# The norm factors of three stages: a transposing DMA of 16-bit halves in place of two TensorE transposes each

## The chip, the cores and the metric

The kernel runs on one core of a Trainium2 chip. Its metric is the device time of one execution in microseconds. Before the change the median of three executions is 600.08 us (600.06 to 600.45). A fourth execution, with the hardware profiler on, took 600.72 us; all rows below are from that one.

## The reference

A trunk of two decoder layers over 256 positions of 1024 features, in float32. Each sub-layer is normalised and added to its input:

```python
def rms_norm(x, g):
    xf = x.astype(jnp.float32)
    y = xf * lax.rsqrt(jnp.mean(xf * xf, axis=-1, keepdims=True) + RMS_EPS)
    return (y * g.astype(jnp.float32)).astype(x.dtype)
...
def swiglu(h, w13, w2):
    g, u = jnp.split(h @ w13, 2, axis=-1)
    return ((jax.nn.silu(g) * u) @ w2).astype(h.dtype)
...
for layer in range(DEPTH):
    y = rms_norm(h, norm_mix[layer])
...
        y = hgrn2_mixer(y, hgrn_w_in[idx], hgrn_w_out[idx], lb_all[idx], hgrn_out_norm[idx])
...
        y = moba_mixer(y, moba_w_in[idx], moba_w_out[idx], rel_bias_table)
    h = h + y
    h = h + swiglu(rms_norm(h, norm_ffn[layer]), ffn_w13[layer], ffn_w2[layer])
return rms_norm(h, final_norm)
```

The part of `rms_norm` that matters here is the factor `rsqrt(mean(x*x) + eps)`: one number for each of the 256 positions.

## The kernel before

**The products.** The activations lie with features on the partitions (`hT`, eight blocks of 128 features by 256 positions). Every float32 operand is split into a high and a low part (`whi`, `wlo`, `xh`, `xl`), and each product is three TensorE matmuls, hi x hi, lo x hi and hi x lo. Weights come in chunks of 128 x 1024 by a DMA on SP's queue into a `raw` slot (some into `ii` or `bt`); ScalarE (ACT) writes `whi` (L496), VectorE (DVE) writes `wlo` (L501). Both have six buffers. A buffer is taken again when TensorE (PE) is done with its last content.

**The norm.** The norm's factor is not multiplied into the activations ahead of a projection: the projection runs on the raw activations, and its result is multiplied by the factor afterwards. `Stats.finish` makes the factor. DVE adds the squares, PE sums them over the partitions, DVE forms mean plus epsilon (`nv`, L753), POOL takes the power -1/2 (`ny`, L756: 128 partitions by 2, position on the partition). Where positions lie along the free axis, the same 256 numbers are needed in every partition: `rrow`, 128 x 256. For that PE transposes each of the two columns of `ny`, broadcast over 128 columns, against the identity into a PSUM bank (L761), and ACT copies the bank to `rrow` (L769). There are five norms. Three of them are touched here:

- `st1`, ahead of the FFN of layer 0 (at 150 to 170 us of the span),
- `st2`, ahead of the attention of layer 1 (330 to 350 us),
- `st3`, ahead of the FFN of layer 1 (420 to 445 us).

**An FFN.** It begins with `first_four`: four output blocks j = 0 to 3, gate and up side by side in one PSUM bank each, over all eight feature blocks k; the last two, k = 6 and 7, are done block by block, so that the four banks are finished one after another. Then block j = 4 follows in one bank, and so on. Four banks of a group exist (`psA` in layer 0, `psB` in layer 1), so j = 4 takes the bank of j = 0 when that one has been read. Bank j is read by `hidden`: DVE multiplies the gate by `rrow` (L1336, into `sgq`), ACT takes the Silu (L1338; it loads its table first), DVE multiplies the up half by that (L1344, into `uu`). For j = 0 to 3 both DVE instructions read the PSUM bank itself; from j = 4 on ACT copies the bank first (`gu`). The first matmul of j = 4 has an operand named `again`, by which it is found in the trace. From j = 5 on the blocks are combined in pairs in a Strassen scheme, in which a weight chunk is fetched with an accumulating DMA on POOL's queue (L545, after `wsum`, L537).

**The order.** The program is written by a planner (`Order`). Operations are put in with an engine, a modelled cost and a due time; the planner keeps a modelled clock of each engine and emits, for each, the ready operation that is due first. The hardware then runs each engine's list strictly in that order. SP's list holds the DMAs; a DMA that waits for its data holds up those behind it.

**An existing transposing DMA.** In layer 1's FFN `flip_h` already turns the eight blocks of `hT` in this manner: ACT copies a block as 16-bit halves (L1618, `flat`), SP issues a DMA that transposes it (L1621, `turns`), and ACT puts the halves together again (L1623, into `ii`).

Of the kernel before, what the change touches and what calls it, by code (L numbers as in the profile page):

```python
# [12 lines left out]
U16 = mybir.dt.uint16  # L13
# [327 lines left out]
def hybrid_trunk(ctx: ExitStack, tc: tile.TileContext, wts, xT, par, gfin, tab, masks, out):  # L341
# [368 lines left out]
    class Stats:  # L710
# [28 lines left out]
                od.op("V", cv(512), lambda: V.tensor_tensor(a.tile, a.tile, s.tile, op=OP.add), reads=[s, a], writes=[a],  # L739
                      due=due)  # L740

        def finish(self, g, due, pow_cost=500, settle=None, place=None):
            a = self.acc
            b = bank(g)
            od.op("V", cv(S), lambda: V.tensor_tensor(a[:, :S], a[:, :S], a[:, S:], op=OP.add), reads=[a], writes=[a],
                  due=due)

            def sums():
                for tt in range(2):
                    mm(b[:, tt:tt + 1], a[:, tt * P:tt * P + P], ones, start=(tt == 0), stop=True)  # L750
            od.op("T", 430, sums, reads=[a], alloc=[b], due=due, early=700.0)
            v = new("nv", [P, 2], 2)
            od.op("V", 80, lambda: V.tensor_scalar(v.tile, b[:, :2], 1.0 / D, EPS, op0=OP.mult, op1=OP.add),  # L753
                  reads=[b], alloc=[v], due=due - 40)
            self.col = y = new("ny", [P, 2], 4)
            od.op("G", pow_cost, lambda: G.tensor_tensor(y.tile, v.tile, mhalf, op=OP.pow), reads=[v], alloc=[y], due=due)  # L756
            c = bank(g)

            def spread():
                for tt in range(2):  # L760
                    T.transpose(c[:, tt * P:tt * P + P], y[:, tt:tt + 1].to_broadcast([P, P]), ident)  # L761
                if settle:
                    x = settle().h.tile
                    mm(c[:, S:S + 2], x[:, :P], x[:, :2], start=True, stop=True)
            o = od.op("T", 220, spread, reads=[y], alloc=[c], due=due, early=700.0)
            if place:
                o.deps.append(place)
            self.row = r = new("rrow", [P, S], 2)
            od.op("A", ca(S), lambda: A.activation(r.tile, c[:, :S], AF.Copy), reads=[c], alloc=[r], due=due - 40)  # L769

    def residual(i, b, x, g, stats, row, due):

        h2 = hT[:, 2 * i:2 * i + 2, :]
        flat = lambda: b[:, :].rearrange("p (j t) -> p j t", j=2)
        if row is not None:
            t = new("yt", [P, 2, S], 2)
            od.op("V", cv(512), lambda: V.tensor_tensor(t.tile, flat(), row.tile.unsqueeze(1).to_broadcast([P, 2, S]),
                                                        op=OP.mult), reads=[b, row], alloc=[t], due=due)
            od.op("V", cv(512), lambda: V.tensor_tensor(h2, t.tile, h2, op=OP.add), reads=[t], writes=hb[2 * i:2 * i + 2], due=due)
        else:  # L780
            od.op("V", cv(512), lambda: V.tensor_tensor(h2, flat(), h2, op=OP.add), reads=[b], writes=hb[2 * i:2 * i + 2], due=due)
        for k in (2 * i, 2 * i + 1):
            split_x(x, k, g, due)
        stats.add(lambda: h2.rearrange("p j t -> p (j t)"), 512, hb[2 * i:2 * i + 2], due + 8)

    def out_rows(name, layer, k, us, banks, nk, done, begin=None):

# [409 lines left out]
        out_rows("hgrn_w_out", 0, k, us, banks, KT, lambda i: residual(i, banks[i], x1, 2, st1, sto.row, 4 * i),  # L1197
                 twin if k == KT // 2 else None)
    twin.free()
    class Place:  # L1200


        end = None

    place = Place()
    st1.finish("B", 30, place=place)

# [24 lines left out]
    def first_four(layer, bk, x, hidden):  # L1234

        for k in range(KT - 2):
            w = {}
            keep["from"] = ws["sub"]
            for j in range(4):
                for half in range(2):  # L1240
                    w[j, half] = piece("ffn_w13", layer, k, half * DFF + P * j, P)
                    o = bk[j][:, half * S:half * S + S]
                    mm(o, w[j, half].hi, x[k].hi, start=(k == 0 and half == 0))
                    od.main(MM)
                    mm(o, w[j, half].lo, x[k].hi)
                    od.main(MM, .67)
                    place.end = 0.0 if (j, half) == (3, 0) else None
                    od.pump()
            for j in range(4):
                for half in range(2):  # L1250
                    mm(bk[j][:, half * S:half * S + S], w[j, half].hi, x[k].lo)
                    od.main(MM, .33)
                od.pump()
            keep["from"] = None
            free_subs(ws["sub"])
        for j in range(4):
            for half in range(2):
                for k in (KT - 2, KT - 1):
                    mm_w(bk[j][:, half * S:half * S + S], piece("ffn_w13", layer, k, half * DFF + P * j, P), x[k],
                         stop=(k == KT - 1))  # L1260
            wrote(bk[j])
            hidden(j, bk[j])
            bk[j].held = False
# [234 lines left out]
    od.need(lambda: 0.0 if extra[1] is None else od.done(extra[1]))  # L1498


    st2.finish("B", 40, 1400)

    vsplit = {}

# [97 lines left out]
        out_rows("moba_w_out", 0, k, ao, banks3, KT, lambda i: residual(i, banks3[i], x3, 3, st3, None, 4 * i))  # L1602


    st3.finish("A", 14)
    for i in (1, 2):
        rings["raw"].slots.append([bt.tile[:, D * i:D * i + D], None, True])
    gf = Buf(None)
# [1 line left out]
    od.op("S", 60, lambda: A.dma_start(gf.tile, gfin.to_broadcast([P, D])), writes=[bt], nbytes=524288, due=60)  # L1610
    ht = new("ii", [P, 2, D])

    words = lambda t: t.bitcast(U16)

    def flip_h(k):

# [159 lines left out]
```

## Time and profile before

| | |
|---|---|
| median of three executions | 600.08 us |
| the profiled execution | 600.72 us |
| its span, first to last instruction | 598.9 us |
| TensorE (PE) busy | 590.1 us, 99% |
| VectorE (DVE) busy | 514.9 us, 86% |
| ScalarE (ACT) busy | 419.3 us, 70% |
| granted TensorE clock, mean | 0.997 |

A matmul's record is longer than the distance to the next one, because matmuls are pipelined: a 128x256 matmul is shown with 0.28 us and the next begins 0.11 us later. What a matmul costs TensorE is therefore read from the distance of starts, not from the durations. ACT and DVE records overlap likewise by about 0.1 us. Times in the rows count from the start of the span.

### The profile page before, as it was taken

The numbers are of one execution on the slowest core, as the hardware profiler recorded it, in microseconds if no ns is written. First come the engines' busy times: TensorE is split into PE (matmuls) and PEld (weight loads), VectorE is DVE, ScalarE is ACT, GpSimd is POOL, SyncE is SP. The second block draws the span as 40 slices with busy tenths as digits, with TensorE's granted clock in tenths as the row PEclk, the third lists the DMA queues.
The fourth block names the chain that finished last, engine by engine and source line by source line (L and its number), as shares of the span: only waits on it lengthen the run. The fifth ranks groups of instructions, "written<-read, shape, count | busy, mean of one in ns | idle before, by whom it ended". The sixth has DMA issues, their size and how long they took to land.

```text
span 598.9 us, 12002 instructions
## 1 busy us (share of the span) xinstructions
PE 590.1 (99%) x4483; PEld 561.7 (94%) x4483; DVE 514.9 (86%) x936; ACT 419.3 (70%) x824; POOL 60.5 (10%) x111
## 2 busy tenths in 40 slices
PE   8999999999999999999999999999999999999995
PEld 7899999999999999999988899999999999999984
DVE  5999988869897888889999678876799888898985
ACT  6898998957676566666838566655788766666763
POOL 0043131501100000000000100000000000000003
PEclk9999999999999999999999999999999999999998
DMA  8956552555888777777666764445678977777611
GB/s 268 371 170 192 176 170 91 164 178 192 247 178 242 225 232 237 222 223 230 232 188 201 244 225 147 157 154 183 189 175 245 315 231 235 235 232 228 205 36 71
DMA packets 43218, 121.84 MB, mean 203 GB/s; under 512 B 9304, under 2 KB 14168, under 8 KB 43160
## 3 DMA queue, kind: packets, MB, share of 16 engines
q1 hardware_dynamic: 39816, 111.61, 56.1%
q0 software_dynamic: 2384, 8.72, 9.0%
q10 hardware_dynamic: 960, 0.76, 0.4%
q8 instruction: 35, 0.57, 0.4%
q14 instruction: 23, 0.19, 0.1%
HBM read 118.64 MB, written 1.38 MB: 200 GB/s over the span
## 4 chain that ended last, share of the span: by engine, by line
PE 98%; DMA 1%; DVE 0%; ACT 0%; SPq 0%; issue 0%; DVEq 0%; ACTq 0%
PE psB L589 50%; PE psA L589 47%; DMA raw<-in_w_dram 1%; PE psB L1570 0%; PE psB L1474 0%; PE psA L761 0%; DVE raw L1653 0%; PE psB L761 0%; ACT whi L489 0%; SPq L520 0%; SPq L675 0%; DVE raw L1709 0%; ACT fa L1680 0%; DVEq L1772 0%; ACT sq L1656 0%
## 5 line engine op out<-in xcount | busy, mean ns | idle before, releaser
L501 DVE TENSOR_TENSOR wlo<-raw,whi 128x1024 fp32r<-128x1024 f32 (+2 forms) x187 | 220.3, 1195 | 24.5 <-ACT whi L496 22.9
L496 ACT ACTIVATE whi<-raw 128x1024 fp32r<-128x1024 f32 (+1 forms) x185 | 187.7, 1036 | 35.6 <-PE psA L589 22.6
L589 PE MATMUL psB<-xh,whi 128*128 128x256 f32 x602 | 169.7, 285 | 0.0
L589 PE MATMUL psB<-xh,wlo 128*128 128x256 f32 x602 | 164.9, 277 | 0.0
L589 PE MATMUL psB<-xl,whi 128*128 128x256 f32 x602 | 160.5, 277 | 0.0
L589 PE MATMUL psA<-xh,whi 128*128 128x256 f32 x539 | 148.0, 278 | 0.0
L589 PE MATMUL psA<-xh,wlo 128*128 128x256 f32 x539 | 147.0, 276 | 0.0
L589 PE MATMUL psA<-xl,whi 128*128 128x256 f32 x539 | 142.1, 276 | 0.0
L589 PEld LDWEIGHTS psB<-xh,wlo 128*128 128x128 f32 x602 | 113.3, 188 | 0.5
L589 PEld LDWEIGHTS psB<-xh,whi 128*128 128x128 f32 x602 | 113.3, 188 | 0.5
L589 PEld LDWEIGHTS psB<-xl,whi 128*128 128x128 f32 x602 | 110.4, 188 | 0.0
L589 PEld LDWEIGHTS psA<-xh,wlo 128*128 128x128 f32 x539 | 101.3, 188 | 0.5
L589 PEld LDWEIGHTS psA<-xh,whi 128*128 128x128 f32 x539 | 101.2, 188 | 0.5
L589 PEld LDWEIGHTS psA<-xl,whi 128*128 128x128 f32 x539 | 98.1, 188 | 0.0
L589 PE MATMUL psB<-whi,hx 128*128 128x512 f32 x174 | 60.0, 391 | 0.0
L589 PE MATMUL psA<-whi,hx 128*128 128x512 f32 (+1 forms) x150 | 51.9, 379 | 0.0
L589 PEld LDWEIGHTS psB<-whi,hx 128*128 128x128 f32 x174 | 32.6, 188 | 6.4
L589 PE MATMUL psB<-wlo,hx 128*128 128x512 f32 x87 | 34.1, 392 | 0.0
L1338 ACT ACTIVATE sgq<-sgq 128x256 f32<-128x256 f32 x44 | 18.3, 415 | 22.1 <-DVE sgq L1336 21.9
L589 PEld LDWEIGHTS psA<-whi,hx 128*128 128x128 f32 x150 | 27.7, 188 | 4.3
L545 POOL DMA_DIRECT2D raw<-in_w_dram x13 | 11.3, 871 | 196.9 <-DVE wsum L537 155.4
L1334 ACT ACTIVATE gu<-psA 128x512 f32<-128x512 f32 x18 | 10.8, 598 | 27.2 <-PE psA L589 27.2
(247 smaller groups left out, 947.8 us busy)
## 6 DMA issues: line engine op xcount, KB each, us to landing
raw<-in_w_dram SPq DMA_DIRECT2D x176, 512.0 KB, 4.3
bt<-in_w_dram SPq DMA_DIRECT2D x15, 512.0 KB, 4.9
raw<-in_w_dram POOLq DMA_DIRECT2D x13, 512.0 KB, 6.0
ii<-in_w_dram SPq DMA_DIRECT2D x9, 512.0 KB, 4.6
raw<-in_w_dram SPq DMA_DIRECT2D x7, 256.0 KB, 5.7
hT<-in_x_dram SPq DMA_DIRECT2D x8, 128.0 KB, 5.5
bt<-scr SPq DMA_DIRECT2D x16, 64.0 KB, 6.1
bt<-in_w_dram POOLq DMA_DIRECT2D x2, 512.0 KB, 6.6
```

Of the source, the lines that this page charges most:

```text
L496: oa = od.op("A", ca(n), lambda h=h, r=src, o=o, n=n: A.activation(h[:, :n], r[:, o:o + n], AF.Copy), reads=[src], alloc=[h], due=due)
L501: V.tensor_tensor(lo[:, c:c + m], r[:, o + c:o + c + m], h[:, c:c + m].bitcast(FT), op=OP.subtract)
L545: od.op("G", 1000, lambda: nc.gpsimd.dma_start(b.tile, wts[c0 // CHUNK], accum_op=OP.add), writes=[b], nbytes=2 * 524288, due=due + 1)
L589: T.matmul(o, a, b, start=start, stop=stop, skip_group_check=True)
L1334: od.op("A", ca(512), lambda b=b: A.activation(g.tile, b[:, :], AF.Copy), reads=[b], alloc=[g], due=0)
L1338: od.op("A", ca(S), lambda: A.activation(s.tile, s.tile, AF.Silu), reads=[s], writes=[s], due=due)
```

## The change

For `st1`, `st2` and `st3` the two transposes on PE, their PSUM bank and the copy of it are left out. In their place ACT copies the two float32 columns of `ny`, seen as four columns of 16-bit halves, each broadcast over 128 columns, into a tile of the ring `sgq`; SP issues a DMA that transposes the four 128 x 128 blocks into a tile of the ring `u`; ACT copies that to `rrow`, putting the halves of each number side by side again. The values are moved bit by bit. The due time of `st1`'s operations goes from 30 to 24, and a device that held `st1`'s transposes back to a set place among the matmuls (`Place`) is left out. The other two norms, one ahead of the mixer of layer 0 and one in it, keep their transposes.

```diff
-        def finish(self, g, due, pow_cost=500, settle=None, place=None):
+        def finish(self, g, due, pow_cost=500, settle=None, turned=False):
...
             od.op("G", pow_cost, lambda: G.tensor_tensor(y.tile, v.tile, mhalf, op=OP.pow), reads=[v], alloc=[y], due=due)
+            self.row = r = new("rrow", [P, S], 2)
+            if turned:
+                s, d = new("sgq", [P, S], 3), new("u", [P, S], 3)
+                od.op("A", ca(512), lambda: A.activation(words(s.tile).rearrange("p (z t) -> p z t", z=4),
+                                                         words(y.tile).unsqueeze(2).to_broadcast([P, 4, P]), AF.Copy),
+                      reads=[y], alloc=[s], due=due - 40)
+                od.op("S", 60, lambda: nc.sync.dma_start(words(d.tile).rearrange("p (z t) -> p z t", z=4), words(s.tile),
+                                                         transpose=True), reads=[s], alloc=[d], nbytes=131072, due=due - 40)
+                od.op("A", ca(512), lambda: A.activation(words(r.tile).rearrange("p (a t z) -> p a t z", a=2, z=2),
+                                                         words(d.tile).rearrange("p (a z t) -> p a t z", a=2, z=2), AF.Copy),
+                      reads=[d], alloc=[r], due=due - 40)
+                return
             c = bank(g)
...
-            o = od.op("T", 220, spread, reads=[y], alloc=[c], due=due, early=700.0)
-            if place:
-                o.deps.append(place)
-            self.row = r = new("rrow", [P, S], 2)
+            od.op("T", 220, spread, reads=[y], alloc=[c], due=due, early=700.0)
...
-    st1.finish("B", 30, place=place)
+    st1.finish("B", 24, turned=True)
...
-    st2.finish("B", 40, 1400)
+    st2.finish("B", 40, 1400, turned=True)
...
-    st3.finish("A", 14)
+    st3.finish("A", 14, turned=True)
```

The order changes around the three places. Line numbers grow by 4 behind `finish` (L1336 becomes L1340, L1338 L1342, L1344 L1348).

ACT's list at the first matmuls of layer 0's FFN, before; `raw_86` to `raw_90` and `ii` are weight chunks, and the last row but one loads the table of Silu:

```order
L496 ACTIVATE whi<-raw_88 128x1024
L496 ACTIVATE whi<-ii 128x1024
L769 ACTIVATE rrow<-psB 128x256
L496 ACTIVATE whi<-raw_89 128x1024
L496 ACTIVATE whi<-raw_90 128x1024
L1338 ACT_TABLE_LOAD
L1338 ACTIVATE sgq<-sgq 128x256
```

The same place of ACT's list in the changed kernel:

```order
L496 ACTIVATE whi<-raw_88 128x1024
L760 ACTIVATE sgq<-ny 128x512
L496 ACTIVATE whi<-ii 128x1024
L765 ACTIVATE rrow<-u 128x512
L496 ACTIVATE whi<-raw_89 128x1024
L496 ACTIVATE whi<-raw_90 128x1024
L1342 ACT_TABLE_LOAD
L1342 ACTIVATE sgq<-sgq 128x256
```

The copy out stands ahead of the split of chunk `ii`, the copy back where the copy from PSUM stood; two splits and the table still lie between it and the first Silu.

DVE's list at the same place, before:

```order
L1295 TENSOR_SCALAR fm<-ny 128x2
L537 TENSOR_TENSOR wsum<-raw_91,raw_86 128x1024
L501 TENSOR_TENSOR wlo<-ii,whi 128x1024
L501 TENSOR_TENSOR wlo<-raw_89,whi 128x1024
L1336 TENSOR_TENSOR sgq<-psA,rrow 128x256
L501 TENSOR_TENSOR wlo<-raw_90,whi 128x1024
L1344 TENSOR_TENSOR uu<-psA,sgq 128x256
```

DVE's list there in the changed kernel:

```order
L1299 TENSOR_SCALAR fm<-ny 128x2
L537 TENSOR_TENSOR wsum<-raw_91,raw_86 128x1024
L501 TENSOR_TENSOR wlo<-ii,whi 128x1024
L1340 TENSOR_TENSOR sgq<-psA,rrow 128x256
L501 TENSOR_TENSOR wlo<-raw_89,whi 128x1024
L501 TENSOR_TENSOR wlo<-raw_90,whi 128x1024
L1348 TENSOR_TENSOR uu<-psA,sgq 128x256
```

The first product with `rrow` moved ahead of one split (L501); the product that frees the bank of j = 0 stays behind all of them.

SP's list at that place in the changed kernel:

```order
L520 DMA raw_86<-in_w_dram 128x1024
L520 DMA raw_87<-in_w_dram 128x1024
L763 DMA_TRANSPOSE u<-sgq 128x4x128
L520 DMA raw_88<-in_w_dram 128x1024
L520 DMA ii<-in_w_dram 128x1024
```

The transposing DMA is new; the four weight loads around it stand in the order of before.

## Rows read from the trace of the kernel before

**Rows 1.** The page: the span, the busy time of each engine with its share and instructions, and the chain that ended last by engine.

```profile
span 598.9 us, 12002 instructions
PE 590.1 (99%) x4483; PEld 561.7 (94%) x4483; DVE 514.9 (86%) x936; ACT 419.3 (70%) x824; POOL 60.5 (10%) x111
PE 98%; DMA 1%; DVE 0%; ACT 0%; SPq 0%; issue 0%; DVEq 0%; ACTq 0%
```

**Rows 2.** The waits of PE over the whole span: who waited for whom, us in total, times, longest.

```profile
PE psA L589 <- DVE mhalf L640: 1.1, 1, 1.1
PE psB L589 <- ACT whi L489: 0.7, 1, 0.7
```

**Rows 3.** PE's timeline around the two transposes of `st1`, of `st2` and of `st3` (start, duration, engine, line, operation and operands, count).

```profile
155.02 0.28 PE L589 MATMUL psA<-xh,whi 128*128 128x256 f32 x1
155.13 0.28 PE L589 MATMUL psA<-xh,wlo 128*128 128x256 f32 x1
155.25 0.38 PE L761 MATMUL psB<-ident,ny 128*128 128x128 f32 x2
...
155.59 0.28 PE L589 MATMUL psA<-xh,wlo 128*128 128x256 f32 x1
...
332.07 0.39 PE L589 MATMUL psA<-whi,xh 128*128 128x512 f32 x1
332.30 0.40 PE L589 MATMUL psA<-wlo,xh 128*128 128x512 f32 x1
332.53 0.38 PE L761 MATMUL psB<-ident,ny 128*128 128x128 f32 x2
...
332.99 0.40 PE L589 MATMUL psA<-whi,xh 128*128 128x512 f32 x1
...
426.97 0.62 PE L589 MATMUL psB<-xl,whi 128*128 128x256 f32 x4
427.43 0.38 PE L761 MATMUL psA<-ident,ny 128*128 128x128 f32 x2
427.56 0.72 PE L589 MATMUL psB<-xl,whi 128*128 128x256 f32 x4
428.12 0.28 PE L589 MATMUL psB<-xh,whi 128*128 128x256 f32 x1
```

**Rows 4.** From the page, DVE's splits of weight chunks with their count, busy time and mean in ns; then ACT's timeline at the first matmuls of layer 0's FFN (in brackets the idle time before it and what ended it).

```profile
L501 DVE TENSOR_TENSOR wlo<-raw,whi 128x1024 fp32r<-128x1024 f32 (+2 forms) x187 | 220.3, 1195 | 24.5 <-ACT whi L496 22.9
...
150.67 1.06 ACT L496 ACTIVATE whi<-ii 128x1024 fp32r<-128x1024 f32 x1 [0.50 <-PE psA L589]
155.67 0.39 ACT L769 ACTIVATE rrow<-psB 128x256 f32<-128x256 f32 x1 [3.93 <-PE psB L761]
155.95 2.00 ACT L496 ACTIVATE whi<-raw 128x1024 fp32r<-128x1024 f32 x2
157.97 1.28 ACT L1338 ACT_TABLE_LOAD   x1
159.26 0.42 ACT L1338 ACTIVATE sgq<-sgq 128x256 f32<-128x256 f32 x1
```

**Rows 5.** The same place on POOL, DVE and PE: the power and the accumulating DMA of POOL, DVE from the first reader of `ny` on, and the first matmul of block j = 4.

```profile
152.43 1.63 POOL L756 TENSOR_TENSOR ny<-nv,mhalf 128x2 f32<-128x2 f32 x1 [11.64 <-DVE nv L753]
155.70 0.94 POOL L545 DMA_DIRECT2D raw<-in_w_dram  x1 [1.64 <-DVE wsum L537]
...
154.09 0.17 DVE L1295 TENSOR_SCALAR fm<-ny 128x2 f32<-128x2 f32 x1 [0.62 <-POOL ny L756]
159.71 0.42 DVE L1344 TENSOR_TENSOR uu<-psA,sgq 128x256 f32<-128x256 f32 x1
...
162.07 0.28 PE L589 MATMUL psA<-again,whi 128*128 128x256 f32 x1
```

**Rows 6.** The existing transposing DMAs: the copies out and back and the DMAs themselves (duration min/median/max in ns, first and last start), the time from issue to landing of all eight, that of the one issued at 434.0, and the DMA that POOL issued beside it.

```profile
L1618 ACT ACTIVATE flat<-hT x8: 613/616/623, 417.6 to 462.1; 128x512 uint16<-128x512 uint16 x8
L1623 ACT ACTIVATE ii<-turns x8: 670/678/695, 424.0 to 472.2; 128x512 uint16<-128x512 uint16 x8
DMA to landing us min/median/max: 2.4/2.7/8.2
...
L1621 SPq DMA_TRANSPOSE turns<-flat x1: 1189/1189/1189, 434.0 to 434.0; - x1
DMA to landing us min/median/max: 8.2/8.2/8.2
...
433.94 0.90 POOL L545 DMA_DIRECT2D raw<-in_w_dram  x1 [7.38 <-DVE wsum L537]
```

**Rows 7.** Layer 1's FFN: SP's loads behind the power, ACT and DVE up to the product that frees the bank of j = 0, and the first matmul of j = 4.

```profile
426.52 0.99 SPq L520 DMA_DIRECT2D raw<-in_w_dram  x2
...
432.72 0.69 ACT L1623 ACTIVATE ii<-turns 128x512 uint16<-128x512 uint16 x1 [1.49 <-DMA turns<-flat]
437.15 0.42 ACT L1338 ACTIVATE sgq<-sgq 128x256 f32<-128x256 f32 x1
...
437.60 0.43 DVE L1344 TENSOR_TENSOR uu<-psB,sgq 128x256 f32<-128x256 f32 x1 [0.91 <-ACT sgq L1338]
...
439.01 0.28 PE L589 MATMUL psB<-again,whi 128*128 128x256 f32 x1
```

**Rows 8.** The place of `st2`: the power on POOL, and the first product with its `rrow` on DVE.

```profile
329.61 2.76 POOL L756 TENSOR_TENSOR ny<-nv,mhalf 128x2 f32<-128x2 f32 x1 [49.83 <-DVE nv L753]
...
344.57 0.42 DVE L1526 SCALAR_TENSOR_TENSOR sgf<-psA,rrow 128x256 f32<-128x256 f32 x1
```

More of the change, by code (lines that the diff above doesn't have):

```diff
@@ L784, in residual @@
         stats.add(lambda: h2.rearrange("p j t -> p (j t)"), 512, hb[2 * i:2 * i + 2], due + 8)
+    words = lambda t: t.bitcast(U16)
     def out_rows(name, layer, k, us, banks, nk, done, begin=None):
@@ L1199, in hybrid_trunk @@
     twin.free()
-    class Place:
-        end = None
-    place = Place()
-    st1.finish("B", 30, place=place)
+    st1.finish("B", 24, turned=True)
     scr = dr.tile([P, NOH], FT, name="scr")
@@ L1246, in first_four @@
                     od.main(MM, .67)
-                    place.end = 0.0 if (j, half) == (3, 0) else None
                     od.pump()
@@ L1611, in hybrid_trunk @@
     ht = new("ii", [P, 2, D])
-    words = lambda t: t.bitcast(U16)
     def flip_h(k):
```

## The prediction

> **What bounds the kernel now.** I read four views, from the whole to the place. First the page: TensorE (PE) is busy for 590.1 of 598.9 us, and the chain that ended last is 98% PE [rows 1]. Then the waits of PE: two in the whole span, of 1.1 and 0.7 us, for things at its start (a constant and the first weights) [rows 2]. From the first matmul to the last PE waits for nobody. So time is gained only by what is taken from PE's list, and lost only where the change makes PE wait. Third, PE's timeline at the three places, to price what goes [rows 3]. Fourth, ACT, DVE and POOL there, to find who is late next [rows 4, 5, 7, 8].
>
> **What goes: six transposes.** A 0.38 us record for a pair is no price, since matmuls overlap; I take distances of starts [rows 3]. At `st1` the matmul at 155.13 and the one at 155.59 have one matmul and the pair between them: 0.46 us. Two matmuls alone take 2 x 0.114 (155.02 to 155.13 is one such step, and a matmul of 512 columns takes 332.07 to 332.30, twice that), so the pair costs 0.46 - 0.23 = 0.23. At `st2`, 332.30 to 332.99 is 0.69 with two steps of 0.23 in it: the pair costs 0.23. At `st3`, 426.97 to 428.12 is 1.15 with eight steps of 0.114 (0.91) in it: 0.24. Together 0.70 us, all of it on PE, the engine that sets the end. The PSUM bank and ACT's three copies of 0.39 us [rows 4] go too; these lay beside PE's work and give nothing by themselves.
>
> One rule speaks against the trade, and nothing below needs it. By the Trainium skill, VectorE: DVE Perf Modes, section The three transpose paths, a 128x128 transpose in bf16 takes 390 ns on TensorE and 1309 ns by the DMA's crossbar, and the same page's Rules for kernel authors send it to TensorE if PSUM will do as its place. An estimate by that page, one such difference at each of three places and all of it on the path, is 3 x 0.92 = 2.8 us lost less the 0.70: 2.1 us slower. The rows charge PE 0.12 us for one transpose and not 0.39, so they differ on that price; on whose path the DMA lies the page says nothing.
>
> **What comes: a longer way to the factor.** After `ny`: a copy out on ACT, 0.62 us, a DMA, 2.4 to 8.2 us to landing, and a copy back on ACT, 0.68 us, all from the same three steps of `flip_h` [rows 6]. That makes 3.7 us at the least. In the kernel before, the way from `ny` (154.06) to the end of the copy from PSUM (155.67 + 0.39 = 156.06) takes 2.0 us at `st1` [rows 4, 5]. The factor is therefore late by some 1.7 us there, and the question is whether PE notices.
>
> *`st1`.* Who waits for it: `hidden` of j = 0, whose second product (159.71 to 160.13) frees the bank that j = 4 takes at 162.07 [rows 5]. The slack is 1.94 us. In the changed kernel, on the old clock: ACT waits for `ny` until 154.09, when DVE's reader of it starts, and copies out until 154.71. SP, whose loads around it wait for other things, issues at about 154.75. I take the quiet landing, 2.4 us, to 157.15, since at that moment the weight load ahead in SP's list has been under way for some time. The copy back starts at 157.2. It is longer than the copy from PSUM by 0.29 us, so what follows starts 0.28 + 0.29 = 0.57 later (before, 155.67 to 155.95 is 0.28). Two splits and the table load take 155.95 to 159.26 = 3.31 as before [rows 4]. Silu starts at 157.2 + 0.57 + 3.31 = 161.08 and ends at 161.50; the product that frees the bank runs 161.53 to 161.95. DVE's second split, moved ahead of that product, needs ACT's second split (ends at 159.8), takes 1.2 us and is done by 161.1, so it isn't the last. PE, 0.23 us earlier by its own transposes, asks for the bank at 161.84. It waits 0.1 us; with the median landing of 2.7 us, 0.4. I take 0.3. Bounds: nothing if the bank is free by some 0.2 us less than I count, 5.9 if the DMA lands as late as the worst row (below).
>
> What else is queued behind the new waits at `st1`: ACT's split of chunk `ii`, done at 150.67 before, moves to 154.7, as it stands behind the copy out. By the six buffers it is the chunk of j = 4's up half, which PE reaches at 162.07 plus 24 steps of 0.114 = 164.8, and its low part, a DVE split of 1.2 us [rows 4], is done by 157.1: covered by over 7 us. The load of `raw_88` behind the DMA goes out 2.5 us later, and the two loads after `ii` some 2 us later; they are for chunks that lie further back still. These I cost at nothing; if that cover were gone, each would cost its 2 us.
>
> *`st2`.* `ny` is done at 329.61 + 2.76 = 332.37 and first needed, as a row, at 344.57 [rows 8]: 12.2 us for a way of 3.7, or 9.5 with the worst landing. No wait. ACT's copy back stands between two groups of evacuations and shifts them by some 0.6 us; the banks are not asked for that early. Nothing.
>
> *`st3`.* The DMA goes out behind the two loads of 426.52 to 427.51 [rows 7], and in its queue it comes after their data, to land by about 432 instead of 430. In the kernel before ACT sat idle for 1.49 us until 432.72, waiting for one of `flip_h`'s DMAs, so the copy back fits in that gap; that DMA of `flip_h` can go out before its old time, as ACT's copy for it stood behind the copy from PSUM and a split. The table load and Silu then keep their place (437.15), and so does the product of j = 0 (437.60 to 438.03) though one split now stands ahead of its first half. j = 4 starts at 439.01, 0.24 earlier with the change: slack 0.98 - 0.24 = 0.74 us. No wait, up to 0.7 us of lateness.
>
> **The sum.** -0.70 + 0.3 = -0.4 us. The profiled execution took 600.72 us (span 598.9 and 1.8 around it): 600.3. The median of the plain runs is 0.64 lower: 600.08 - 0.4 = 599.7 us. What this measurement can tell from no change is about 0.2%, 1.2 us; the whole 0.70 is less than that.
>
> **Rivals.**
>
> *A: the full gain.* PE finds the bank of j = 4 free. For it: my wait is 0.1 to 0.4 us, less than several steps of it are known to. Against it: every step is in the rows, and the slack of 1.94 is all but used up. 600.08 - 0.70 = 599.4 us.
>
> *B: the DMA at `st1` lands late, and PE stands at j = 4: slower.* One mechanism, one place: the transposing DMA shares the DMA engines with the accumulating load of POOL. The row for it is the transposing DMA issued at 434.0 beside POOL's load of 433.94: it landed after 8.2 us, where the median is 2.7 [rows 6]. At `st1` POOL issues such a load at 155.70 [rows 5], 1 us behind the new DMA. With 8.2 us the row's copy starts at 163.0, Silu at 166.9, the freeing product ends at 167.75, and PE waits 167.75 - 161.84 = 5.9 us: 600.08 - 0.70 + 5.9 = 605.3. It decides from a landing of 4.2 us on, where the wait of 1.9 us makes +1.2. Against it: at 434.0 both began together behind a weight load of SP, and here the DMA has a lead of 1 us and the load ahead of it has been issued longer; it should be through when POOL's data come. Landings between 3.1 and 4.2 us give a wait of 0.8 to 1.9 and a time of 600.2 to 601.3.
>
> *C: late at all three places.* If the 1.7 us by which the way grows at `st1` reached PE at each place, 3 x 1.7 - 0.70 = 4.4 us: 604.5. For it: the way is longer at each. Against it: a slack of 12.2 us at `st2` and of 1.94 at `st1`. (The Trainium skill's rule above leads here.)
>
> *D: the slots on PE aren't freed.* If matmul steps stretch by what was taken away, nothing changes: 600.1. No row shows PE held by anything but its own list.
>
> **How the numbers follow.** The forecast (a wait of 0.1 to 0.6 at `st1`): 0.45. A: 0.25. B: 0.11 past the point of 4.2 us, and 0.12 between 0.6 and 1.9 us of wait. C: 0.02. D: 0.05. The likeliest gives 599.7, by itself 599.4 to 600.0. The range takes in A with a few tenths for the run to run spread (600.06 to 600.45), and late landings up to a wait of some 2 us: 599.1 to 601.5; most of what is left out is B. Faster by over 0.2% would need more than all that is taken from PE; I leave it 0.03 out of A's chance. Slower by over 0.2%: B past its point and C, 0.13. Within 0.2%: 0.84.
>
> **What would show it.** Right: no transposes of `ny` at the three places and steps of 0.114 through them; in PE's waits at most one new entry, at the first `again` matmul of layer 0's FFN, for DVE's product, of a few tenths; `rrow` at `st1` written from 157.2 to 157.9 and Silu at about 161.1; no wait of PE near 344 or 439. Wrong: a landing at `st1` over 3 us with a longer wait of PE (B); a wait at 439, which would mean that the DMA behind two loads lands after 433; or a chunk's split late for PE further on, which would mean that I misjudged the cover of the moved loads.

## The result: 0.7% slower, with a late landing at `st1`

The changed kernel takes 604.82 us (median of 12 runs, 600.58 to 607.88), the kernel before, on the same chip, 600.30 us (12 runs, 599.78 to 600.95). The ratio is 1.0072, with a 95% interval of 1.0051 to 1.0094. I had forecast 599.7 us, with 601.5 at the upper end. What came is rival B by its mechanism, a late landing at `st1`, with a second cost that I had not counted; that the median also lies near B's price (605.3) is partly luck, as told below. The twelve runs of the changed kernel spread over 7 us where those before spread over one.

The profiled execution is the slowest of the twelve, 607.88 us with a span of 606.0, so what follows accounts for that one; the median run has no trace. From the page (span, busy time, the clock granted to TensorE in 40 slices, and the chain that ended last, by engine and by line; the last row is the clock of the kernel before):

```profile
span 606.0 us, 11998 instructions
PE 592.0 (98%) x4477; PEld 563.6 (93%) x4477; DVE 514.7 (85%) x936; ACT 422.0 (70%) x827; POOL 60.8 (10%) x111
...
PEclk9999999999989999999999999999999999999998
...
PE 88%; DMA 3%; issue 3%; ACT 3%; DVE 1%; POOL 1%; SPq 0%; DVEq 0%; ACTq 0%; POOLq 0%
PE psB L589 45%; PE psA L589 42%; DMA u<-sgq 2%; ACT whi L496 1%; DMA raw<-in_w_dram 1%; DMA turns<-flat 1%; PE psB L1574 0%; DVE wlo L501 0%; ACT xh L703 0%; DVE xl L705 0%; PE psB L1478 0%; POOL ny L756 0%; POOL again L1167 0%; ACT L1342 0%; SPq L520 0%
...
PEclk9999999999999999999999999999999999999998
```

Beside [rows 1] the chain has gone from 98% PE to 88%, and the new DMA, `u<-sgq`, holds 2% of it. The clock has one digit that the kernel before doesn't have, the 8 in slice 12, which is 167 to 182 us; the 8 of the last slice stands in both. PE's waits (who waited for whom; us in total, times, longest), beside [rows 2]:

```profile
PE psA L589 <- DVE uu L1348: 4.5, 1, 4.5
...
PE psB L589 <- ACT whi L496: 0.5, 1, 0.5
PE psB L589 <- DVE uu L1348: 0.4, 1, 0.4
```

Three entries are new. The one of 0.5 us lies at the start, at 8.9 us, far ahead of the change. The other two are a bank waiting for a product of `hidden`: 4.5 us at j = 4 of layer 0 (`st1`), 0.4 us at j = 4 of layer 1 (`st3`). The timelines at `st1` (ACT, SP, POOL, PE; start, duration, in brackets idle time and what ended it), beside [rows 4, 5]:

```profile
154.17 0.63 ACT L760 ACTIVATE sgq<-ny 128x512 uint16<-128x512 uint16 x1 [3.91 <-POOL ny L756]
161.62 0.69 ACT L765 ACTIVATE rrow<-u 128x512 uint16<-128x512 uint16 x1 [5.87 <-DMA u<-sgq]
165.52 0.42 ACT L1342 ACTIVATE sgq<-sgq 128x256 f32<-128x256 f32 x1
...
154.83 2.17 SPq L763 DMA_TRANSPOSE u<-sgq  x1
...
155.78 0.94 POOL L545 DMA_DIRECT2D raw<-in_w_dram  x1 [1.64 <-DVE wsum L537]
...
166.54 0.55 PE L589 MATMUL psA<-again,whi 128*128 128x256 f32 x1 [4.47 <-DVE uu L1348]
166.89 0.42 PE L589 MATMUL psA<-again,wlo 128*128 128x256 f32 x1
167.10 0.41 PE L589 MATMUL psA<-again,whi 128*128 128x256 f32 x1
```

The DMA goes out at 154.83, as I had it (154.75), and POOL's load 0.95 us behind it. But `rrow` is written from 161.62, a landing of 6.8 us, not from 157.2. All that hangs on it is as long as forecast: Silu 3.90 behind the start of `rrow` (forecast 161.08 - 157.2 = 3.88). The price is in PE's last three rows. It stands for 4.47 us, and then its steps are 0.21 us (166.89 to 167.10) in place of 0.114. The clock by stretches (PE's busy time and matmuls, granted clock, DMA share, GB/s) says why:

```profile
160.00:162.00 2.00, 2.00 (x19) 1.00 0.93 291
162.00:164.00 2.00, 0.07 (x1) 1.00 0.67 274
164.00:166.00 2.00, 0.00 (x0) 0.66 0.27 37
166.00:168.00 2.00, 1.46 (x7) 0.50 0.98 277
168.00:170.00 2.00, 2.00 (x11) 0.50 0.80 249
170.00:172.00 2.00, 2.00 (x13) 0.63 0.69 59
172.00:174.00 2.00, 2.00 (x19) 1.00 0.79 89
```

The granted clock falls to half at 164.65 and comes back at 171.48 (the clock's own record in the trace). From 166.54 on that costs half of 4.94 us, 2.5 us.

I lined up every matmul of the two traces by its operands and followed the difference of starts. Set against a common start, the trace of after gains 0.25 us at the pair of `st1`, loses 4.63 by the wait and 2.75 behind it (2.5 by the clock, the rest by steps of 0.118 us after it), gains 0.24 at `st2` and 0.24 at `st3`, and loses 0.64 at j = 4 of layer 1. The sum is 7.29 us, and the spans differ by 606.0 - 598.9 = 7.1. The median run is 4.5 us slower than before; how that divides is not shown.

At `st3`, beside [rows 7] (SP, ACT, PE):

```profile
434.24 0.99 SPq L520 DMA_DIRECT2D raw<-in_w_dram  x2
435.33 1.19 SPq L763 DMA_TRANSPOSE u<-sgq  x1
...
440.27 0.69 ACT L765 ACTIVATE rrow<-u 128x512 uint16<-128x512 uint16 x1 [1.88 <-DMA u<-sgq]
...
446.30 0.36 PE L589 MATMUL psB<-again,whi 128*128 128x256 f32 x1 [0.40 <-DVE uu L1348]
```

The DMA goes out behind the two loads, as I had said, and lands after 4.9 us. On the clock of before (less the 6.73 us by which PE is late there) that is 433.5, not "about 432", and the wait is 0.40 us: the forecast's own sign of error, a landing after 433 with a wait at 439.

### The profile page after: what moved, and what is told of

It reads as the page before. It is cut to its first block, busy times and chain, and to the rows that moved or that the text cites. A ratio compares the mean times of both kernels' runs of the same rounds, so it can differ in the third digit from the quotient of the medians.

```text
span 606.0 us, 11998 instructions
## 1 busy us (share of the span) xinstructions
PE 592.0 (98%) x4477; PEld 563.6 (93%) x4477; DVE 514.7 (85%) x936; ACT 422.0 (70%) x827; POOL 60.8 (10%) x111
## 4 chain that ended last, share of the span: by engine, by line
PE 88%; DMA 3%; issue 3%; ACT 3%; DVE 1%; POOL 1%; SPq 0%; DVEq 0%; ACTq 0%; POOLq 0%
PE psB L589 45%; PE psA L589 42%; DMA u<-sgq 2%; ACT whi L496 1%; DMA raw<-in_w_dram 1%; DMA turns<-flat 1%; PE psB L1574 0%; DVE wlo L501 0%; ACT xh L703 0%; DVE xl L705 0%; PE psB L1478 0%; POOL ny L756 0%; POOL again L1167 0%; ACT L1342 0%; SPq L520 0%
## 5 line engine op out<-in xcount | busy, mean ns | idle before, releaser
L501 DVE TENSOR_TENSOR wlo<-raw,whi 128x1024 fp32r<-128x1024 f32 (+2 forms) x187 | 220.7, 1198 | 24.0 <-ACT whi L496 22.3
L1342 ACT ACTIVATE sgq<-sgq 128x256 f32<-128x256 f32 x44 | 18.1, 415 | 22.1 <-DVE sgq L1340 22.1
L1340 DVE TENSOR_TENSOR sgq<-gu,rrow 128x256 f32<-128x256 f32 x36 | 15.2, 423 | 17.6 <-ACT gu L1338 17.6
```

What stands on the lines that cost most here:

```text
L501: V.tensor_tensor(lo[:, c:c + m], r[:, o + c:o + c + m], h[:, c:c + m].bitcast(FT), op=OP.subtract)
L1340: od.op("V", cv(S), lambda: V.tensor_tensor(s.tile, b[:, :S], row.tile, op=OP.mult), reads=[b, row], alloc=[s], due=due)
L1342: od.op("A", ca(S), lambda: A.activation(s.tile, s.tile, AF.Silu), reads=[s], writes=[s], due=due)
```

## The experiments

"Before" stands for the runs of the kernel before made beside each group of kernels: 600.35 us for e1 to e4, 600.43 for e5 to e7, 600.67 for e8 to e11, 600.46 for e12 to e14.

**Which place loses.** e3 takes `st1` back to two transposes and leaves `st2` and `st3` turned; e4 is the other half.

```
e3:  - st1.finish("B", 24, turned=True)
     + st1.finish("B", 30, place=place)
     ... (with the class Place and its use put back)
e4:  - st2.finish("B", 40, 1400, turned=True)
     + st2.finish("B", 40, 1400)
     - st3.finish("A", 14, turned=True)
     + st3.finish("A", 14)
```

> st1 keeps its two TensorE transposes, their place and due time of before; st2 and st3 are turned by DMA as in the changed kernel. If the loss is st1's alone: before less 0.47 us (two pairs of transposes) plus the wait of up to 0.6 us that the changed kernel shows at the first j = 4 matmul of layer 1: 599.8 to 600.5 us, runs within 1 us of each other. If the loss comes from late factors at all three places (rival C): 602 us or more.

> Only st1 is turned by DMA; st2 and st3 keep their transposes. If the loss is st1's alone: the changed kernel's time to within 0.7 us, 604 to 605.5 us, with the same spread from run to run (over 4 us), and PE's wait at j = 4 of layer 0 of 3 us or more. If it comes from all three: a third of the loss, near 602.

e3: 600.62 us (600.1 to 601.76), ratio 1.0005 [0.9996, 1.0014], 0.1 us over what was expected, and rival C falls. e4: 605.97 us, ratio 1.0069 [1.0039, 1.0099], and its eight runs fall into two groups: 600.99, 601.17 and 602.42, then five from 605.84 to 607.69. So the loss that stands clear of the noise is at `st1`, and it doesn't come in every run. In e4's profiled run the landing was 5.4 us and PE's wait 3.1.

**Is it POOL's load?** e1 and e5 hold POOL's first accumulating load behind a copy of two columns that reads `rrow`; e1 put them into a small tile of its own, which moved the tiles behind it in memory, e5 into columns of one that exists. e2 leaves the load where it is but doesn't accumulate (it leaves out one weight chunk of a sum).

```
e1:  + mark = sb.tile([P, 2], FT, name="mark")
     + od.op("G", 700, lambda: G.tensor_copy(mark, rows1[0][:, :2]), reads=[rows1[0]], due=due)
       od.op("G", 1000, lambda: nc.gpsimd.dma_start(..., accum_op=OP.add), ...)   (now behind the copy)
     ... (for the first of these loads only)
e5:  the same, with lead[:, 64:66] in place of mark
e2:  - nc.gpsimd.dma_start(b.tile, wts[c0 // CHUNK], accum_op=OP.add)
     + nc.gpsimd.dma_start(b.tile, wts[c0 // CHUNK])   (for the first of these loads only)
```

> The changed kernel, with one thing moved: the first accumulating load on POOL's queue in layer 0's FFN stands behind a copy of 2 elements that reads rrow, so that it goes out only when st1's transposing DMA has landed. Theory 1 (that load, 1 us behind the transposing DMA, holds back its landing): the DMA lands 2.4 to 3.5 us after issue instead of 6.8, Silu of j = 0 starts at 161 to 162, PE waits under 1.2 us at the first matmul of j = 4, no stretch of halved clock, 599.6 to 601.0 us. Rival 2 (the DMA is late for its own sake or for SP's loads ahead of it): landing stays at 5 us or more, PE waits over 3 us, 603 us or more.

> The changed kernel, but the first load on POOL's queue in layer 0's FFN is a plain one that doesn't accumulate (left out: the sum of one weight chunk). Same place, same bytes read and written to the same slot. Theory 1a (it is the accumulating that holds the transposing DMA back): landing 2.4 to 3.5 us, under 1.2 us of wait, 599.6 to 601.0. Theory 1b (any load on that queue 1 us behind it does): landing over 5 us as in the changed kernel, 603 us or more. Rival 2 (the DMA is late for its own sake): also 603 or more, so 1b and 2 are told apart by the late load.

> GpSimd's first accumulating load of layer 0's FFN is again held until the row of factors of st1 is there, but the small marker goes into columns of a tile that exists already, so that no tile of the kernel moves in memory. Theory 1 (the accumulating load of 155.8 us holds back the completion of the transposing DMA, and that wait with the clock loss behind it is the whole price; the long matmul steps of e1 came of the extra tile): landing 2.4 to 3.5 us, TensorE's wait ahead of j = 4 at most 1 us, granted clock 1.0 at 164 to 172 us, no stretch of matmul steps 4% longer before 152 us, and 599.6 to 600.9 us (3 x 0.24 us gained, 0.5 to 0.9 us back at st3 and st1). Rival (the long steps belong to the held load, or to chance): the landing is as short, and the time stays at 602 to 602.9 us as in e1. Rival (the landing is late whatever GpSimd does): landing over 5 us, 604 us and more.

e1: landing 2.5 us, no wait of PE at j = 4, no half clock; yet 602.34 us (602.08 to 602.85), over theory 1's upper end of 601.0. Its trace shows steps of 0.118 us from 133 us on, long before `st1`, to 162, and again at 340 to 355 and 428 to 439. e5, with the tiles where they were, has none of these before `st1` and takes 601.34 us (600.7 to 602.3), ratio 1.0013 [1.0004, 1.0022]: 0.4 us over the upper end of what theory 1 gave, and 3.5 us below the changed kernel. Its timelines at `st1` (SP, ACT, POOL):

```profile
154.77 1.32 SPq L767 DMA_TRANSPOSE u<-sgq  x1
...
158.35 0.69 ACT L769 ACTIVATE rrow<-u 128x512 uint16<-128x512 uint16 x1 [2.65 <-DMA u<-sgq]
...
159.11 0.18 POOL L548 COPY lead<-rrow 128x2 f32<-128x2 f32 x1 [5.02 <-ACT rrow L769]
159.75 0.94 POOL L549 DMA_DIRECT2D raw<-in_w_dram  x1 [0.46 <-DVE sgq L1345]
```

With POOL's load out of the way the landing is 3.6 us, PE's wait 1.3, and the clock stays at 1.0. e2: 603.48 us (601.3 to 605.08), landing 3.9, wait 1.6, between what theories 1a and 1b expected: with a plain load in the same place the transfer is still late. Its packets are shorter (0.21 us on average for 4096 bytes, 0.39 for the accumulating ones of the changed kernel), but the times of e2 are not better than those of e10 below (602.69), which accumulates. So the long delays need POOL's load behind the DMA: with it held, none of 27 runs (e1, e5, e7) is above 603.54. But the load alone doesn't make the landing late, as e6 and e13 show below, and e5's 3.6 us is not e1's 2.5.

**Does the idle time take the clock down?** e6 puts sixteen matmuls of ones in front of j = 4 in the changed kernel. e8, e9 and e12 go to the kernel before, in which no DMA transposes near this place (its first one, `flip_h`'s, is some 250 us later): POOL computes powers, and one small matmul ahead of j = 4 reads them. e8 has six powers, e12 twelve, and e9 has e8's six and twenty-four matmuls to fill the gap.

```
e6:  ... + for _ in range(16): mm(wb[:, :P], ones128, ones128, start=True, stop=True)
e8:  ... + G.tensor_copy(t, rows1[0][:, :2])
     + for _ in range(6): G.tensor_tensor(t, t, mhalf, op=OP.pow)
     ... + mm(wb[:, :2], ones128, lead[:, 64:66], start=True, stop=True)   (lead[:, 64:66] is t)
e9:  e8, and 24 matmuls as in e6 ahead of the last line
e12: e8 with range(12)
```

> The changed kernel with sixteen matmuls of ones (128x128, fp32, into a bank that is free) added on TensorE just ahead of j = 4 of layer 0's FFN, where it waits; nothing of the kernel reads their product. Theory 2 (the half clock at 165 to 171 us comes of TensorE's idle time of 4.5 us): the landing stays at 5 to 7 us and rrow comes as late, but the granted clock holds 1.0 at 164 to 172 us, the matmul steps there keep 0.114 us, and the loss at st1 falls from 7.2 us by the 2.4 us of the clock: 602.5 to 605.5 us, no run above 606. Rival (the half clock has another cause, such as the transposing DMA itself): the steps behind j = 4 are still 0.2 us for some 4 us, and the time is that of the changed kernel, 604 to 608 us.

> The kernel before, with no transposing DMA at all, and a wait put in by hand: GpSimd computes six powers of two columns one after the other behind its load at 155.7 us (1.63 us each by the row at 152.43 us, so until some 167 us), and one small matmul on TensorE just ahead of j = 4 of layer 0's FFN reads their result; nothing else uses it. TensorE so stands idle from 162.2 us for 4 to 5 us. Theory 2 (idle time of TensorE past some 2.7 us takes the clock down): a stretch of half clock begins some 2.7 us behind the start of the gap and lasts some 6.8 us, steps of 0.2 us behind j = 4, and the whole costs 4.5 us of idle time and 2 to 2.5 us of clock: 606 to 608 us. Rival (the half clock belongs to the transposing DMA or to what it does to the transfers): steps of 0.114 us right behind the gap, 604 to 605.5 us.

> e8 with twenty-four matmuls of ones (128x128, fp32, some 0.21 us each by e6) ahead of the small one, so that TensorE works through the gap of e8. Theory 2: as late at j = 4 as e8 by 4.5 to 5.2 us, with the granted clock at 1.0 throughout: 604.8 to 605.7 us, 1 to 3 us below e8. Rival: the same time as e8 within 0.7 us.

> e8 with twelve powers on GpSimd in place of six: they took 0.95 us each there, so the last ends at some 167 to 168 us and TensorE stands idle for 4.5 to 6 us ahead of j = 4 of layer 0's FFN, in the kernel before, with no transposing DMA. In the runs so far gaps of 1.3 and 1.6 us left the granted clock at 1.0, and gaps of 2.6, 3.1 and 4.5 us were followed by one, one and two stretches of 3.41 us at half clock. Theory 2: one or two such stretches here too, matmul steps of 0.2 us in them, and a time of 606 to 609 us (the gap's 4.5 to 6 us and 1.2 to 2.5 us of clock). Rival (the half clock belongs to the transposing DMA): full clock behind the gap, 604.5 to 606.5 us.

e6: 603.79 us, and no run of it above 604.02 where the changed kernel reaches 607.88. But in its profiled run the DMA landed after 2.6 us, so there was no gap to fill and the sixteen matmuls were plain cost (3.4 us): it doesn't tell the theories apart. e8 doesn't either: one power took 0.95 us and not 1.63, the gap was 0.4 us, and 601.37 us is below both expectations. e9, built for e8's gap, so measures its matmuls alone: 606.23 us, at full clock. e12 tells. PE's first matmul behind the gap, and the clock (columns as above):

```profile
167.39 0.58 PE L590 MATMUL psB<-lead,ones 128*128 128x2 f32 x2 [5.81 <-POOL lead L1301]
...
162.00:164.00 2.00, 0.00 (x0) 1.00 1.02 380
164.00:166.00 2.00, 0.00 (x0) 0.76 0.78 63
166.00:168.00 2.00, 0.61 (x3) 0.50 0.73 139
168.00:170.00 2.00, 2.00 (x10) 0.50 0.40 156
170.00:172.00 2.00, 2.00 (x12) 0.54 0.00 0
```

With no transposing DMA at this place, a gap of 5.8 us is followed by the same 6.83 us of half clock: 608.81 us (608.37 to 609.81), ratio 1.0145. The powers themselves don't do it, as six of them in e8 left the clock at 1.0. So the half clock comes of the idle time and doesn't need the DMA. Its record has a grain: the half stretches are 6.83 us long in the changed kernel and in e12, and 3.41 us, half of that, in e4 (gap 3.1 us) and e10 (gap 2.6). Gaps of 1.3 us (e5) and 1.6 us (e2) left it at 1.0. This agrees with the Trainium skill, TensorE: Matmul & The Clock Gate, section What's actually happening, which gives a window of 3413 ns that runs freely. The same page's section Why this matters for your kernels warns of gaps over some 3 us; here 2.6 us was enough for one window, and the measurement decides.

The place of the gap counts too. In every trace the granted clock, counted from the first record of full clock, changes only at whole multiples of 3.41 us. Laid on that grid, the idle time falls into its windows thus: the changed kernel 2.6 and 1.9 us (two windows at half clock follow), e12 3.4 and 2.4 (two), e4 2.7 and 0.4 (one), e10 0.6 and 2.0 (one), e2 1.6 (none), e5 1.3 (none). So 2.0 us in one window was enough and 1.6 was not. The mean granted clock, which is on record for every run, shows how often it happened. It is 0.996 or more in every run of the kernel before beside the experiments. It is lower in 7 of the changed kernel's 12 runs (two at 0.991, like the profiled one, and five at 0.993 to 0.995), in 4 of 8 of e4, 2 of 8 of e10, 2 of 6 of e2 and all 4 of e12, and in no run of any other kernel, the 27 with the load held among them.

**Why is the landing 2.5 us in some kernels and 5 to 7 in others?** In e6 POOL's load went out 0.95 us behind the DMA, exactly as in the changed kernel, and the landing was 2.6 us. e10 was to hold the load by one power; it failed, since the power ran at 154.23, while the load was still waiting for DVE, and the load went out 0.95 us behind the DMA as ever. It so stands as a near repeat of the changed kernel. In the records of the transfers I then saw a 16 KB instruction fetch beside the DMA's packets in the late kernels. e13 moves the fetch: eight matmuls of two columns at the start shift PE's code by 32 instructions. e14 is e13 with `st3` on PE.

```
e10: + od.op("G", 1700, lambda: G.tensor_tensor(lead[:, 64:66], ones128[:, :2], mhalf, op=OP.pow), ...)
       (ahead of the accumulating load)
e13: + for _ in range(8): mm(wb[:, :2], ones128, ones128[:, :2], start=True, stop=True)
       (behind the eight matmuls of ones at the start)
```

> The changed kernel with one power of two columns (1.63 us) put on GpSimd just ahead of its first accumulating load of layer 0's FFN, which so goes out at 157.3 to 157.6 us in place of 155.8, 2.6 us or so behind the transposing DMA. Theory 1, sharper (it is a race of half a microsecond: the completion writes of the transposing DMA get out at once if GpSimd's packets are not there when its own are through, some 1.5 to 2.5 us behind its issue, and some 3 us late otherwise): landing 2.5 to 3.7 us, no half clock, 600.7 to 602.3 us as in e5. Rival (any accumulating load that starts before the row of factors is there delays it): landing over 5 us, 603 us and more.

> The changed kernel with eight matmuls of two columns put in at its very start, where TensorE waits for the first load for 0.7 us; they move nothing later but TensorE's code by 32 instructions (16 KB of code lasts it some 14 us, so its fetches come some 1.8 us earlier against its work). Theory 1c: in the changed kernel and in e4, e5 and e10 a fetch of 16 KB lay across the packets of the transposing DMA, which took 1.0 to 1.6 us instead of 0.8, and the landing was 3.6 us (no GpSimd load near) or 5.0 to 6.8 us (its packets came in between); in e1, e6 and e7 it lay ahead of them and the landing was 2.5 to 2.6 us. With the fetch moved ahead: landing 2.4 to 2.8 us though GpSimd's load goes out 0.95 us behind the DMA as ever, TensorE's wait at st1 at most 0.4 us, no half clock, 600 to 601.5 us. Rival (the fetch is a bystander, GpSimd's load alone decides): landing 5 to 7 us, 603 to 607 us.

> e13 with st3 back on TensorE. Theory 1c: 0 to 0.6 us below e13, 599.6 to 601 us. Rival: as e13's rival, 603 us and more.

e10: 602.69 us (601.63 to 605.15), landing 4.9, PE's wait 2.6, one window of half clock in its slowest run, which is the profiled one: near the rival's landing, but no test of the hold. e13, SP, ACT and POOL at `st1` and PE's wait:

```profile
158.70 1.32 SPq L765 DMA_TRANSPOSE u<-sgq  x1
...
161.24 0.69 ACT L767 ACTIVATE rrow<-u 128x512 uint16<-128x512 uint16 x1 [1.61 <-DMA u<-sgq]
...
159.65 0.94 POOL L545 DMA_DIRECT2D raw<-in_w_dram  x1 [1.64 <-DVE wsum L537]
...
PE psA L589 <- DVE uu L1350: 0.2, 1, 0.2
```

The landing is 2.5 us with POOL's load 0.95 us behind the DMA, and PE waits 0.2 us. Its time, 605.27 us, is no measure of that: in its trace full clock came at 12.4 us and not at 4.2, and PE ran 4 us late from there on; one run of six, 601.32 us, is 4 us below the rest. The small matmuls alone don't explain it, since e14 has the same ones and its trace has full clock at 4.2 us. e14: 602.45 us (601.76 to 606.38), landing 3.3, wait 1.0; three of its seven runs are at 605.8 to 606.4, and which of the two losses they had is not shown. It missed theory 1c's range of 599.6 to 601.

The records of the transfers in ten kernels (us; read packet by packet from the trace of each). The DMA moves 512 packets of 256 bytes and then 32 writes of 4 bytes, which I take for its completion: in all ten the landing follows the last of them by 0.3 to 0.6 us.

| kernel | DMA issued | its packets | fetch of 16 KB | longest packet | POOL's first packet | completion writes | landing | PE's wait |
|---|---|---|---|---|---|---|---|---|
| after | 154.83 | 156.12 to 157.38 | 155.59 to 156.57 | 0.61 | 157.43 | 160.1 to 161.1 | 6.8 | 4.5 |
| e4 | 154.80 | 156.08 to 157.19 | 155.42 to 156.31 | 0.50 | 157.42 | 159.2 to 159.8 | 5.4 | 3.1 |
| e10 | 154.94 | 156.24 to 157.22 | 155.45 to 156.40 | 0.36 | 157.53 | 158.4 to 159.5 | 4.9 | 2.6 |
| e2, plain | 155.26 | 156.56 to 157.33 | 155.21 to 156.32 | 0.05 | 157.52 | 157.7 to 158.8 | 3.9 | 1.6 |
| e5, held | 154.77 | 156.07 to 157.69 | 155.94 to 156.81 | 1.02 | 161.39 | 156.7 to 157.7 | 3.6 | 1.3 |
| e14 | 154.88 | 156.18 to 157.69 | 154.08 to 155.52 | 0.78 | 157.48 | 156.9 to 157.7 | 3.3 | 1.0 |
| e6 | 154.25 | 155.55 to 156.32 | 154.43 to 155.36 | 0.05 | 156.91 | 156.4 to 156.6 | 2.6 | none |
| e13 | 158.70 | 160.00 to 160.77 | 157.16 to 158.57 | 0.04 | 161.44 | 160.7 to 160.9 | 2.5 | 0.2 |
| e7, held | 154.16 | 155.46 to 156.23 | 154.22 to 155.20 | 0.05 | 159.78 | 156.3 to 156.4 | 2.5 | 0.2 |
| e1, held | 155.56 | 156.87 to 157.64 | 155.62 to 156.55 | 0.05 | 161.18 | 157.6 to 157.8 | 2.5 | none |

Read it from the bottom. Left alone, the packets take 0.77 us and the completion is out 0.1 to 0.3 us later. POOL's first packet comes some 0.6 us behind the last of the DMA's in e6 and e13: that is the whole margin. In e2 no packet stalls, but the plain load is issued faster, its packets come 0.19 us behind, and the writes are late. In the other upper rows four to seven of the 512 packets stall, the longest by 0.36 to 1.02 us, and in the changed kernel, e4 and e10 the margin is used up by it: the 4-byte writes come out only among POOL's packets. In the changed kernel the data packets were through by 157.4, and ACT was told 4 us later. In e5 and e14 the writes had come out by 157.7. So the margin alone doesn't settle it either: in e14 POOL's first packet came 0.2 us ahead of the DMA's last one, and the landing was 3.3 us. In four of the five kernels with a stall the fetch still ran when the DMA's first packets started, by 0.74, 0.45, 0.23 and 0.16 us, and the stalls, 1.02, 0.61, 0.50 and 0.36, go in that order; in the four without a stall whose fetch is near, it had ended 0.2 to 0.3 us before. e14 speaks against the fetch as the only cause: its fetch was 0.66 us gone, and a packet stalled for 0.78 us all the same. Nor is POOL's load what makes the packets stall: in e5 its first packet comes 3.7 us behind them. SP's weight loads, which move beside them, were varied in no run. What holds the DMA's packets there, and why e5 and e14 got 20 or more of the 32 writes out during the stall and the changed kernel none, stays open.

**Is there a version that beats the kernel before?** e7 is e5 with `st3` on PE; e11 is the kernel before with `st2` alone turned.

```
e7:  e5, and  - st3.finish("A", 14, turned=True)   + st3.finish("A", 14)
e11: before, and  - st2.finish("B", 40, 1400)      + st2.finish("B", 40, 1400, turned=True)
```

> As e5, with st3's factors spread by two transposes on TensorE again; st1 and st2 turned by the DMA. Theory 1 (each pair removed gives 0.24 us, st3 gives back 0.6 us, and the held load takes away st1's wait): 0.3 to 0.6 us below e5 where theory 1 holds there, so 599.3 to 600.3 us, 0.2 to 0.8 us below the kernel before. Rival (st3's turn is worth nothing either way): equal to e5 within 0.2 us. Rival (the held load costs by itself): 601 us and more.

> The kernel before with st2 alone turned by the DMA; st1 and st3 stay with two transposes each on TensorE. One pair less is 0.24 us less on TensorE and no wait was seen at st2 in any run: 600.0 to 600.3 us, 0.1 to 0.4 us below the kernel before. Rival (a turn costs something that the trace's waits don't show, as the 0.37 us of longer steps behind st2 in e3): 600.4 to 601 us.

e7: 601.77 us (600.88 to 603.54), ratio 1.0023 [1.0014, 1.0032], no better than e5. e11: 600.75 us, ratio 1.0001 [0.9992, 1.001]. Neither beats it, both lie above what theory 1 and the gain of a pair gave, and both times fall into their rivals' ranges. Lined up matmul by matmul, both show the 0.24 us gained for each pair, and both give it back, with no wait of PE but 0.2 us in e7: steps of 0.118 us at 340 to 350 us (0.36 to 0.38 us), in e7 also behind `st1` (0.4 us); e11 loses some 0.6 us from 439 us on, where nothing was changed, 0.4 of it by such steps. The steps at 340 to 350 us don't belong to the turn of `st2`: e9, which turns nothing, has them, and the changed kernel, e2, e4 and e5 don't, though three of these turn `st2`. With one trace of each kernel, chance from run to run isn't excluded.

## Why the prediction was wrong, point by point

- **What goes** was right: 0.23, 0.23 and 0.24 us by distances of starts, and 0.25, 0.24 and 0.24 measured in the changed kernel (about the same in the others that turn the place; in e1 longer steps lie over it). All of it is PE's time, and rival D (the slots not freed) falls there; that e7 and e11 end no faster has to do with steps elsewhere.
- **The chain from the landing to the bank at `st1`** was right to 0.2 us: from the start of `rrow` the forecast has 161.95 - 157.2 = 4.75 us to the end of the freeing product, and PE's start at 166.54 lies 4.92 behind 161.62.
- **The step that failed** is the landing at `st1`: "I take the quiet landing, 2.4 us", and in the case against B "it should be through when POOL's data come". The data were through, by 0.05 us (157.38 against 157.43). The completion wasn't. Where the landing was quiet (2.5 to 2.6 us in e1, e6, e7 and e13) PE waited 0 to 0.2 us, so the rest of the sum holds. I had compared the end of one transfer with the start of another as if the gap were wide; it was 0.6 us at best and 0.05 in the profiled run. The landing was 6.8 us, and PE waited 4.5 us where I had 0.3. The changed kernel's spread of 7 us looks like this race, won in one run (600.58) and lost by different amounts in the others; e4's two groups of runs and the lower clock in 7 of the 12 runs fit that, but only one run of each kernel has a trace, so it isn't shown. Why the DMA's packets stall, which lets POOL's come first, also stays open.
- **B's price** was close by luck: one term was too large and one was missing. 605.3 came from a wait of 5.9 us; the traces of the changed kernel, e4 and e10 have waits of 2.6 to 4.5 us, and 1.5 to 2.5 us of half clock behind them, a term that stands in none of my cases. The chance of 0.11 was too small for something whose one row in the trace was a landing of 8.2 us beside the same kind of load [rows 6].
- **`st2`**: no wait, as forecast (landing 3.7 us in a slack of 12).
- **`st3`**: the order behind the two loads was right, the landing not: 433.5 on the old clock in place of about 432, so 0.4 us of wait (0.64 by starts) in place of none.
- **The rule on the place of a transpose.** No kernel with `st1` turned is below the kernel before, so the direction that the Trainium skill gives (VectorE: DVE Perf Modes, section Rules for kernel authors) held here. The mechanism was another than one way's price against the other's: with a quick landing (e7) the longer way is nearly hidden.
- **The chances.** A's full gain needed three pairs of 0.24 us and no loss; neither e5, with all three places turned and the load held, nor e7 reaches it.

## What to carry to other kernels

A transposing DMA that replaces work on the busy engine is only as good as its worst landing: look for what is issued within 2 us of it on any queue, and price the completion behind that, not the data. Where a slack of 2 us stands on a landing with a row of 8 us in the same trace, the row is the price until a run says otherwise. And a wait of the busy TensorE that puts 2.0 us or more of idle time into one window of 3.41 us (waits of 2.6 us and more here, not those of 1.6 and less) is to be charged with 1.5 to 2.5 us of half clock on top, by the traces of this case.

## What I had not expected of the hardware

- The completion of a transposing DMA came up to 3.7 us after its last data packet (157.38 to 161.05) with an accumulating load of POOL behind it, and 0.1 to 0.3 us after it in e1, e6, e7 and e13, where the packets didn't stall and POOL's came some 0.6 us or more behind.
- The half clock comes in units of 3.41 us, and one gap of 2.6 us cost one unit, one of 4.5 us two; a unit followed where 2.0 us of the window before was idle.
- Matmul steps of 0.118 us in place of 0.1135, at full granted clock, in stretches of some 10 us; which traces show them and where changes with edits elsewhere (at 340 to 350 us e1, e3, e6, e7, e9, e10, e11, e13 and e14 have them, seven others don't). Over a stretch they cost about 0.4 us, nearly as much as two of the pairs removed. Their cause stays open.
- Full clock came at 12.4 us in the trace of e13 and at 4.2 us in that of e14, with the same eight small matmuls at the start, and it moved all that follows by 4 us.
